# A hybrid encoder block on one core: where the adaLN products stand in the VectorE's list, and which steps of an attention head go first

## The chip, the core and the metric

The kernel runs on one core of a Trainium2 chip. A core has a TensorE (PE in the profile, with PEld for its weight loads), a VectorE (DVE), a ScalarE (ACT), a GpSimd (POOL, not used here but for a constant) and a SyncE (SP), which here issues all the transfers. Each engine works through a list of instructions of its own, in order; semaphores tie the lists together. The metric is the device time of one execution in microseconds.

## What is computed

One layer of an encoder with 256 positions, width 2048 and 16 heads of 128, all in float32:

```python
mod = silu(c) @ w_ada + b_ada
sh1, sc1, gt1, sh2, sc2, gt2, sh3, sc3, gt3 = split(mod, 9)
f = swiglu(modulate(rms_norm(h, g_ffn1), sh1, sc1), w1_gate, w1_up, w1_down)
h = h + 0.5 * gt1 * f
q, k, v = split(modulate(rms_norm(h, g_mix), sh2, sc2) @ w_qkv, 3)
# q and k normed; 8 heads of 2-D neighbourhood attention, 8 of dilated attention
h = h + gt2 * (concat(rms_norm(o_na), rms_norm(o_dil)) @ w_o)
f = swiglu(modulate(rms_norm(h, g_ffn2), sh3, sc3), w2_gate, w2_up, w2_down)
h = h + 0.5 * gt3 * f
```

The hidden width of both feed-forwards is 5632. With only 256 positions every weight is used on few columns, so the weights have to be streamed from memory once: 500 MB, 151 of them for `w_ada` alone.

## The kernel before

Weights come in chunks of 128 x 1024 (eight 128 x 128 blocks, 0.5 MB). To keep float32 accuracy a chunk is cut in two: ACT casts it to a rounded part `hi` (line 157), DVE subtracts it to leave the remainder `lo` (line 158; in the profile the tile is called low). PE then multiplies each block twice (`mm2`, lines 161 to 164): the rounded part by a rounded and a remainder part of the activations together (512 columns), the remainder by the rounded part alone (256 columns). `W.chunk` (lines 304 to 316) fetches and splits three chunks ahead of the one in use (`AHEAD`); raw chunks have five buffers, the two parts four each.

The adaLN vector `mod` is 144 columns of 128 values. Each column is one block of `w_ada`, 128 x 2048 or 1 MB. It does not pass through PE: the transfer (`ada_issue`, line 132) brings it, and one DVE instruction multiplies it by the broadcast of silu(c) and sums each row (`ada_use`, line 140). In the profile its tile is ra (two buffers) or rx (one more, outside attention). The blocks are spread thinly over the weight stream: each chunk that is fetched adds `ws.rate` to a credit, and at 1 a block is issued (lines 308 to 314). The rates are set by stage with `ws.pace`: `RA` and `RB` in the first feed-forward, `RQ` in attention, `RE` and `RF` in the second feed-forward. A block's transfer is kept behind that of the last chunk in SP's list (lines 133, 134); its product is written in the program when a later block needs its place in `pend` (`bg_step`, lines 254 to 258). `hold` keeps products behind the last step of a norm that PE waits for.

A planner arranges the lists: it takes instructions by priority, which is their place in the program, when its own estimate says that they can start. An instruction may so come out ahead of others that stand before it in the program. `high_priority(offset=n)` ranks the instructions within it as if they stood n places earlier. `after` (lines 116 to 120) adds an edge that the planner has to respect, without a semaphore when both are on one engine.

The stages are: first feed-forward (part of the up-projections ahead of time, the rest, down-projection, then the last 12 of 44 hidden blocks in the same way), attention, second feed-forward. In the second feed-forward the 64 chunks of `w2_a` run under `RE`, and 60 of the 64 of `w2_b` under `RF[0]`; `rest2` demands the modulation columns, `gate3` the gates.

In attention, 96 units of the q/k/v projection and 32 of the output projection run one after the other. PE's list there is written out by hand (`manual_schedule`); DVE and ACT are left to the planner. The steps of a head (`head`, lines 627 to 704) are hung on later units by a table `PLAN`: transposes of q and k (a_pe) and their split (a_ew), scores (b_pe), bias, maximum and exponentials (b_ew1), normalising (b_ew2), transposes of the probabilities (c_pe), their split (c_ew), the product with v (d_pe) and the output (d_ew). Norms of q and k (`qk_norm`) and sums of squares (`Stat`) feed the same engines.

Of the kernel before, what the change touches and what calls it, by code (L numbers as in the profile page):

```python
# [9 lines left out]
F32 = mybir.dt.float32  # L10
F32R = mybir.dt.float32r
AF = mybir.ActivationFunctionType
ALU = mybir.AluOpType
AX = mybir.AxisListType
# [24 lines left out]
RA = 0.475  # L39
RB = (0.28, 0.36, 0.36, 0.3)  # L40
RQ = 0.2
RE = 0.25
RF = (0.1, 0.2, 0.1, 0.1)
AHEAD = 3
RAWB = 5
ARA = 2
ARX = 1
LOB = 4
URGENT = 400
LINE = 16  # L50
PLACE = ((12, 36),) + 3 * ((16, 0),) + ((44, 40),) + 3 * ((48, 0),)
MANUAL = {mybir.EngineType.PE}
# [12 lines left out]
def build(tc, a):  # L65
    nc = tc.nc
    with ExitStack() as ctx:
# [44 lines left out]
        hold = []  # L112

        queue = []

        def after(ins, other, why):
            tc.add_manual_dep(
                ins.ins, other.ins.name,
                mybir.DependencyInfo(mybir.DependencyClass.NoSync, mybir.DependencyReason.DATA),
                reason=why)  # L120

        def held(ins):
            if hold:
                after(ins, hold[-1], "hold")

        def ada_issue(i):
            turn[0] += 1
            if wide and turn[0] % (ARA + ARX) >= ARA:
                raw = wide["p"].tile([P, D], F32, tag="arx", bufs=ARX, name=f"rx{i}")
            else:  # L130
                raw = wp.tile([P, D], F32, tag="ara", bufs=ARA, name=f"ra{i}")
            ins = nc.sync.dma_start(raw, a["w_ada"][i])
            if queue:
                after(ins, queue[-1], "queue")
            return raw

        def ada_use(raw, i):
            j, k = i // KT, i % KT
            m = mods[j][:, k : k + 1]
            held(nc.vector.tensor_tensor_reduce(  # L140
                out=raw, in0=raw, in1=cb, scale=1.0, scalar=vec[:, BA + i : BA + i + 1],
                op0=ALU.mult, op1=ALU.add, accum_out=m))
            if j in GAIN:
                g = vec[:, GAIN[j] + k : GAIN[j] + k + 1]
                nc.vector.scalar_tensor_tensor(m, m, 1.0, g, ALU.add, ALU.mult)
# [8 lines left out]
        def wsplit(raw, place):  # L154
            hi = wp.tile([P, CW + 64], F32R, tag="whi", bufs=LOB, name="hiw")[:, place[0] : place[0] + CW]
            lo = wp.tile([P, CW + 64], F32R, tag="wlo", bufs=LOB, name="low")[:, place[1] : place[1] + CW]
            nc.scalar.copy(hi, raw)  # L157
            nc.vector.tensor_tensor(lo, raw, hi.bitcast(F32), ALU.subtract)  # L158
            return hi, lo

        def mm2(out, lh, ll, r, first, last):
# [9 lines left out]
        def split(src, hi, lo):  # L171
            nc.scalar.copy(hi, src)
            nc.vector.tensor_tensor(lo, src, hi.bitcast(F32), ALU.subtract)
# [210 lines left out]
        def ffn(kx, part, ready_k, gate, rates, stat=None, out=None):  # L384


            hid = {}
            head = [pair("pb") for f in range(NF1)]
            ready_k(KM)
            for f in range(NF1):  # L390
                up_mm(head[f], kx, KM, True, False)
            ready_k(KT)
            ws.pace(rates[0])
            for f in range(NF1):
                up_mm(head[f], KM, KT, False, True)
                up_finish(f, head[f], part, hid)
            for f in range(NF1, F1):
                ps = pair("pb")
                up_mm(ps, kx, KT, True, True)
                up_finish(f, ps, part, hid)  # L400
            psum_pool("bank")
            ws.pace(rates[1])
            ffn_down(range(F1), hid, gate)
            psum_pool("pair")
            ws.pace(rates[2])
            for f in range(F1, FT):
                ps = pair("pb")
                up_mm(ps, 0, KT, True, True)
                up_finish(f, ps, {}, hid)
            ln_exp_set()  # L410
            psum_pool("bank")
            ws.pace(rates[3])
            ffn_down(range(F1, FT), hid, gate, stat, out)
# [92 lines left out]
        with tc.tile_pool(name="att", bufs=2) as ap_, tc.tile_pool(name="atc", bufs=1) as ac:  # L506
# [120 lines left out]
            def head(g, i, a0, b0, c0, d0):  # L627
                hd = g * 4 + i
                s_ = {}
                hs = slice(i * P, (i + 1) * P)  # L630

                def a_pe():
                    s_["pT"] = bank("pT")
                    for q, nm in enumerate(("k", "q")):
                        for t in range(2):
                            o_ = q * S + t * P
                            nc.tensor.transpose(s_["pT"][:, o_ : o_ + P], res[g, nm, t][:, i, :], ident)

                def a_ew():
                    s_["th"] = ap_.tile([P, 512], F32R, tag="th", name="th")  # L640
                    s_["tl"] = ap_.tile([P, 512], F32R, tag="tl", name="tl")
                    split(s_["pT"], s_["th"], s_["tl"])

                def b_pe():
                    th, tl = s_["th"], s_["tl"]
                    s_["ps"] = bank("psc").rearrange("p (t s) -> p t s", t=2)
                    for t in range(2):
                        qs = slice(S + t * P, S + (t + 1) * P)
                        mm3(s_["ps"][:, t, :], th[:, qs], tl[:, qs], th[:, 0:S], tl[:, 0:S], True, True)

                def b_ew1():
                    sc = ap_.tile([P, 2, S], F32, tag="sc", name="sc")
                    nc.vector.scalar_tensor_tensor(sc, s_["ps"], HD ** -0.5, s_["bias"], ALU.mult, ALU.add)
                    mx = sp.tile([P, 2], F32, tag="mx", name="mx")
                    nc.vector.tensor_reduce(mx, sc, axis=AX.X, op=ALU.max, negate=True)
                    sm = sp.tile([P, 2], F32, tag="sm", name="sm")
                    for t in range(2):
                        nc.scalar.activation(
                            sc[:, t, :], sc[:, t, :], AF.Exp, bias=mx[:, t : t + 1], accum_out=sm[:, t : t + 1])
                    s_["p"], s_["sm"] = sc, sm  # L660

                def b_ew2():
                    sc, sm = s_["p"], s_["sm"]
                    nc.vector.reciprocal(sm, sm)
                    for t in range(2):
                        if t < PACT:
                            nc.scalar.activation(sc[:, t, :], sc[:, t, :], AF.Copy, scale=sm[:, t : t + 1])
                        else:
                            nc.vector.tensor_scalar(sc[:, t, :], sc[:, t, :], sm[:, t : t + 1], None, ALU.mult)

                def c_pe():
                    s_["pP"] = bank("pP").rearrange("p (t s) -> p t s", t=2)
                    for t in range(2):
                        for kt in range(2):
                            nc.tensor.transpose(
                                s_["pP"][:, kt, t * P : (t + 1) * P], s_["p"][:, t, kt * P : (kt + 1) * P], ident)

                def c_ew():
                    s_["ph"] = ap_.tile([P, 2, S], F32R, tag="ph", name="ph")
                    s_["pl"] = ap_.tile([P, 2, S], F32R, tag="pl", name="pl")  # L680
                    split(s_["pP"], s_["ph"], s_["pl"])

                def d_pe():
                    s_["po"] = bank("po")[:, :S]
                    for kt in range(2):
                        vh, vl = res[g, "v", kt]
                        mm3(s_["po"], vh[:, hs], vl[:, hs], s_["ph"][:, kt, :], s_["pl"][:, kt, :],
                            kt == 0, kt == 1)

                def d_ew():  # L690
                    po = s_["po"]
                    go = vec[:, GO + hd : GO + hd + 1]
                    nc.scalar.activation(ox[hd][:, 0, :], po, AF.Copy, scale=go)
                    nc.vector.scalar_tensor_tensor(
                        ox[hd][:, 1, :], po, go, ox[hd][:, 0, :].bitcast(F32), ALU.mult, ALU.subtract)
                    ost[hd // 8].add(po, False)

                def fetch():
                    s_["bias"] = na_bias(hd) if g < 2 else lnc

                at(max(0, a0 - 2), fetch)
                for u, fn in ((a0, a_pe), (a0 + 1, a_ew), (b0, b_pe), (b0 + 1, b_ew1), (b0 + 2, b_ew2),
                              (c0, c_pe), (c0 + 1, c_ew), (d0, d_pe), (d0 + (0 if d0 == LAST else 1), d_ew)):
                    at(u, fn)
# [161 lines left out]
```

## Time and profile before

| | |
|---|---|
| median of three runs | 1928.16 us (1927.46 to 1933.04) |
| the profiled execution | 1929.37 us, of which the span of its instructions 1927.4 us |
| granted clock of the TensorE, mean over the span | 0.993 |
| memory traffic | 500.09 MB read, 261 GB/s over the span |
| first feed-forward, PE at work | 22 to 769 us |
| attention, projections and output projection | 776 to 1191 us |
| second feed-forward | 1196 to 1924 us |

The profile is that of one execution. A group of it gives line, engine, operation, tile written <- tiles read, shape and count, then busy time and the mean of one in ns, then the idle time of the engine ahead of these instructions and what ended it. The list of waits gives who waited for whom: total, times, longest. The timeline gives start and length of each instruction, those alike put together, with the wait ahead of the first in square brackets. The start of one matmul to that of the next is the better measure of PE, since their ends overlap.

### The profile page before, as it was taken

To read this page: it belongs to the slowest core of one execution; us is meant where nothing else is said; L and a number is where in the kernel's file an instruction comes from. 1 tells how busy PE (TensorE), PEld (TensorE's weight loads), DVE (VectorE), ACT (ScalarE), POOL (GpSimd) and SP (SyncE) were. 2 spreads that over 40 slices of the span, in tenths; PEclk is the share of its full clock that TensorE was granted. 3 is DMA by queue.
4 is the path that set the end of the run, shared out by engine and by line. 5 is a ranking of instruction groups with operands and counts; after the bars stand their busy time and mean duration, and the time that the engine had idled before them with its cause. 6 is when DMAs were issued, how large, how long until landed. Compare 5 with 4: busy or idle time off the path is not lost.

```text
span 1927.4 us, 27567 instructions
## 1 busy us (share of the span) xinstructions
PE 1885.8 (98%) x10564; PEld 1639.3 (85%) x10564; DVE 1565.1 (81%) x2122; ACT 906.8 (47%) x1333; POOL 0.7 (0%) x6
## 2 busy tenths in 40 slices
PE   7999999999999999999999999999999999999999
PEld 5878888888888888887878788888888888888888
DVE  7899999988888889868876799788798976665665
ACT  2444544543334454555555465545454443334442
POOL 0000000000000000000000000000000000000000
PEclk8999999999999999999999999999999999999999
DMA  9998888789998887776755445787677677766664
GB/s 384 383 332 292 299 299 296 295 323 338 330 332 327 312 306 256 246 286 222 263 189 194 145 141 164 273 304 286 230 234 235 210 251 273 260 228 191 193 203 136
DMA packets 120227, 503.98 MB, mean 261 GB/s; under 512 B 13344, under 2 KB 15904, under 8 KB 101664
## 3 DMA queue, kind: packets, MB, share of 16 engines
q1 hardware_dynamic: 120096, 502.24, 74.5%
q8 instruction: 82, 1.34, 0.3%
q14 instruction: 49, 0.40, 0.1%
HBM read 500.09 MB, written 2.10 MB: 261 GB/s over the span
## 4 chain that ended last, share of the span: by engine, by line
PE 85%; DVE 8%; DMA 3%; issue 2%; ACT 2%; SPq 0%; DVEq 0%; ACTq 0%
PE pb L163 20%; PE pd L163 17%; PE pb L164 10%; PE pd L164 8%; PE pa L163 8%; PE pqk L169 4%; PE pa L164 4%; PE pqv L169 3%; DVE low L158 3%; PE pqq L169 3%; DMA ra<-in_w_ada_dram 2%; PE pa L462 2%; PE pso L163 2%; ACT hiw L157 1%; PE pso L164 1%
## 5 line engine op out<-in xcount | busy, mean ns | idle before, releaser
L157 ACT CAST hiw<-rw 128x1024 fp32r<-128x1024 f32 x644 | 674.2, 1049 | 705.1 <-PE pd L163 234.0
L158 DVE TENSOR_TENSOR low<-rw,hiw 128x1024 fp32r<-128x1024 f32 x644 | 782.0, 1221 | 186.5 <-ACT hiw L157 184.5
L163 PE MATMUL pb<-nx,hiw 128*128 128x512 f32 x1920 | 657.4, 390 | 0.0
L164 PE MATMUL pb<-nx,low 128*128 128x256 f32 x1920 | 532.1, 277 | 1.1 <-DVE low L158 1.1
L163 PE MATMUL pd<-hd,hiw 128*128 128x512 f32 x1408 | 481.9, 390 | 0.0
L163 PEld LDWEIGHTS pb<-nx,hiw 128*128 128x128 f32 x1920 | 360.5, 188 | 76.9
L164 PE MATMUL pd<-hd,low 128*128 128x256 f32 x1408 | 390.1, 277 | 1.8 <-DVE low L158 1.8
L164 PEld LDWEIGHTS pb<-nx,low 128*128 128x128 f32 x1920 | 360.9, 188 | 1.9 <-DVE low L158 1.9
L163 PEld LDWEIGHTS pd<-hd,hiw 128*128 128x128 f32 x1408 | 264.3, 188 | 56.3
L140 DVE CUSTOM_DVE_ANT_0 ra<-ra,cb,vec 128x2048 f32<-128x2048 f32 x101 | 237.2, 2349 | 75.2 <-DMA ra<-in_w_ada_dram 75.0
L163 PE MATMUL pa<-nx,hiw 128*128 128x512 f32 x800 | 276.1, 392 | 3.7 <-ACT hiw L157 3.2
L164 PEld LDWEIGHTS pd<-hd,low 128*128 128x128 f32 x1408 | 264.6, 188 | 2.6 <-DVE low L158 2.4
L164 PE MATMUL pa<-nx,low 128*128 128x256 f32 x800 | 221.6, 279 | 4.0 <-DVE low L158 4.0
L163 PEld LDWEIGHTS pa<-nx,hiw 128*128 128x128 f32 x800 | 149.6, 188 | 37.2 <-ACT hiw L157 5.2
L164 PEld LDWEIGHTS pa<-nx,low 128*128 128x128 f32 x800 | 150.4, 188 | 8.9 <-DVE low L158 7.9
L140 DVE CUSTOM_DVE_ANT_0 rx<-rx,cb,vec 128x2048 f32<-128x2048 f32 x43 | 101.0, 2348 | 28.6 <-DMA rx<-in_w_ada_dram 28.3
L163 PE MATMUL pso<-ox,hiw 128*128 128x512 f32 x256 | 92.4, 404 | 0.0
L169 PE MATMUL pqk<-hiw,nx 128*128 128x512 f32 x256 | 85.5, 400 | 0.0
L169 PE MATMUL pqq<-hiw,nx 128*128 128x512 f32 x256 | 84.3, 399 | 0.0
L169 PE MATMUL pqv<-hiw,nx 128*128 128x512 f32 x256 | 81.5, 393 | 0.3 <-ACT nx L232 0.3
L378 DVE SCALAR_TENSOR_TENSOR h<-pd,m,h 128x256 f32<-128x256 f32 x128 | 61.2, 481 | 16.5 <-PE pd L164 14.7
L164 PE MATMUL pso<-ox,low 128*128 128x256 f32 x256 | 72.5, 283 | 0.0
(133 smaller groups left out, 1513.5 us busy)
## 6 DMA issues: line engine op xcount, KB each, us to landing
ra<-in_w_ada_dram SPq DMA_DIRECT2D x101, 1024.0 KB, 7.4
rw<-in_w_b_dram SPq DMA_DIRECT2D x144, 512.0 KB, 4.6
rw<-in_w_d_dram SPq DMA_DIRECT2D x128, 512.0 KB, 5.2
rw<-in_w_a_dram SPq DMA_DIRECT2D x100, 512.0 KB, 4.8
rw<-in_w_c_dram SPq DMA_DIRECT2D x96, 512.0 KB, 4.4
rw<-in_w_qkv_dram SPq DMA_DIRECT2D x96, 512.0 KB, 4.3
rx<-in_w_ada_dram SPq DMA_DIRECT2D x43, 1024.0 KB, 7.3
rw<-in_w_e_dram SPq DMA_DIRECT2D x48, 512.0 KB, 4.4
```

What stands on the lines that cost most here:

```text
L140: held(nc.vector.tensor_tensor_reduce(out=raw, in0=raw, in1=cb, scale=1.0, scalar=vec[:, BA + i : BA + i + 1], op0=ALU.mult, op1=ALU.add, ...
L157: nc.scalar.copy(hi, raw)
L158: nc.vector.tensor_tensor(lo, raw, hi.bitcast(F32), ALU.subtract)
L163: nc.tensor.matmul(out, lh, r, start=first, stop=False)
L164: nc.tensor.matmul(out[:, :S], ll, r[:, 0, :], start=False, stop=last)
L169: nc.tensor.matmul(out, l, r, start=first and i == 0, stop=last and i == 2, **kw)
L378: nc.vector.scalar_tensor_tensor(h[d], part_, g, h[d], ALU.mult, ALU.add)
L462: nc.tensor.matmul(pa[f][:, q, :], w[:, b * P : (b + 1) * P], full[k], start=k == 0 and q == 0, stop=k == K1 - 1 and q == 1, skip_group_ch ...
```

## The change

It has three parts.

1. `wsplit` keeps the last two remainders in `lows`. From the point in the first feed-forward where `late` is set, a block that is issued takes along `lows[0]`, the remainder of the chunk before the one fetched last, and its product gets an edge behind that remainder.
2. Four of a head's element-wise steps (a_ew, b_ew1, b_ew2, c_ew) are put in `high_priority(offset=SOON)`, with `SOON = 60`. The step d_ew is not.
3. In the second feed-forward `RE` is 0.28 in place of 0.25, and `RF[0]` is 0.2 in place of 0.1.

```diff
-RE = 0.25
-RF = (0.1, 0.2, 0.1, 0.1)
+RE = 0.28
+RF = (0.2, 0.2, 0.1, 0.1)
+SOON = 60
...
+        lows = []
+        late = []
...
             ins = nc.sync.dma_start(raw, a["w_ada"][i])
             if queue:
                 after(ins, queue[-1], "queue")
-            return raw
+            return raw, lows[0] if late and lows else None
 
         def ada_use(raw, i):
             j, k = i // KT, i % KT
             m = mods[j][:, k : k + 1]
-            held(nc.vector.tensor_tensor_reduce(
+            raw, low = raw
+            ins = nc.vector.tensor_tensor_reduce(
                 out=raw, in0=raw, in1=cb, scale=1.0, scalar=vec[:, BA + i : BA + i + 1],
-                op0=ALU.mult, op1=ALU.add, accum_out=m))
+                op0=ALU.mult, op1=ALU.add, accum_out=m)
+            held(ins)
+            if low is not None:
+                after(ins, low, "landing")
...
-            nc.vector.tensor_tensor(lo, raw, hi.bitcast(F32), ALU.subtract)
+            lows[:] = lows[-1:] + [nc.vector.tensor_tensor(lo, raw, hi.bitcast(F32), ALU.subtract)]
             return hi, lo
...
             ready_k(KT)
+            late[:] = [True]
             ws.pace(rates[0])
...
                 def a_ew():
-                    s_["th"] = ap_.tile([P, 512], F32R, tag="th", name="th")
-                    s_["tl"] = ap_.tile([P, 512], F32R, tag="tl", name="tl")
-                    split(s_["pT"], s_["th"], s_["tl"])
+                    with tc.high_priority(offset=SOON):
+                        s_["th"] = ap_.tile([P, 512], F32R, tag="th", name="th")
+                        s_["tl"] = ap_.tile([P, 512], F32R, tag="tl", name="tl")
+                        split(s_["pT"], s_["th"], s_["tl"])
...
```

The bodies of b_ew1, b_ew2 and c_ew are indented under the same line; nothing else in them changes.

More of the change, by code (lines that the diff above doesn't have):

```diff
@@ L651, in b_ew1 @@
                 def b_ew1():
[L652 to L659, printed above, removed]
@@ L660, in b_ew1 @@
-                    s_["p"], s_["sm"] = sc, sm
-                def b_ew2():
[L663 to L669, printed above, removed]
+                    with tc.high_priority(offset=SOON):
+                        sc = ap_.tile([P, 2, S], F32, tag="sc", name="sc")
+                        nc.vector.scalar_tensor_tensor(sc, s_["ps"], HD ** -0.5, s_["bias"], ALU.mult, ALU.add)
+                        mx = sp.tile([P, 2], F32, tag="mx", name="mx")
+                        nc.vector.tensor_reduce(mx, sc, axis=AX.X, op=ALU.max, negate=True)
+                        sm = sp.tile([P, 2], F32, tag="sm", name="sm")
+                        for t in range(2):
+                            nc.scalar.activation(
+                                sc[:, t, :], sc[:, t, :], AF.Exp, bias=mx[:, t : t + 1], accum_out=sm[:, t : t + 1])
+                        s_["p"], s_["sm"] = sc, sm
@@ new lines, in b_ew2 @@
+                def b_ew2():
+                    with tc.high_priority(offset=SOON):
+                        sc, sm = s_["p"], s_["sm"]
+                        nc.vector.reciprocal(sm, sm)
+                        for t in range(2):
+                            if t < PACT:
+                                nc.scalar.activation(sc[:, t, :], sc[:, t, :], AF.Copy, scale=sm[:, t : t + 1])
+                            else:
+                                nc.vector.tensor_scalar(sc[:, t, :], sc[:, t, :], sm[:, t : t + 1], None, ALU.mult)
@@ L678, in c_ew @@
                 def c_ew():
-                    s_["ph"] = ap_.tile([P, 2, S], F32R, tag="ph", name="ph")
-                    s_["pl"] = ap_.tile([P, 2, S], F32R, tag="pl", name="pl")
-                    split(s_["pP"], s_["ph"], s_["pl"])
+                    with tc.high_priority(offset=SOON):
+                        s_["ph"] = ap_.tile([P, 2, S], F32R, tag="ph", name="ph")
+                        s_["pl"] = ap_.tile([P, 2, S], F32R, tag="pl", name="pl")
+                        split(s_["pP"], s_["ph"], s_["pl"])
                 def d_pe():
```

## The prediction

> **What bounds the kernel now.** I read the page first, then the stretches by stage, then the list of waits, then the timelines around each place where the TensorE (PE) stood still.
>
> ```profile
> PE 1885.8 (98%) x10564; PEld 1639.3 (85%) x10564; DVE 1565.1 (81%) x2122; ACT 906.8 (47%) x1333; POOL 0.7 (0%) x6
> PE 85%; DVE 8%; DMA 3%; issue 2%; ACT 2%; SPq 0%; DVEq 0%; ACTq 0%
> L158 DVE TENSOR_TENSOR low<-rw,hiw 128x1024 fp32r<-128x1024 f32 x644 | 782.0, 1221 | 186.5 <-ACT hiw L157 184.5
> L140 DVE CUSTOM_DVE_ANT_0 ra<-ra,cb,vec 128x2048 f32<-128x2048 f32 x101 | 237.2, 2349 | 75.2 <-DMA ra<-in_w_ada_dram 75.0
> ```
>
> PE is the bound: busy 98%, 85% of the chain that ended last. Nothing in the change removes PE work, so all there is to gain is the few per cent in which PE waits. DVE is the engine that makes it wait. Its two large jobs are the remainder of a weight chunk (L158, 1.22 us) and the product of an adaLN block (L140, 2.35 us). The product also made DVE stand idle 75 us for its own transfer, and DVE takes its instructions in the order of its list: what stands behind a waiting product waits too. Which stages does that hurt?
>
> ```profile
> 182.00:396.00 214.00, 214.00 (x1252) 188.81 (x1251) 206.53 (x280) 107.55 (x142) 0.00 (x0) 1.00 0.82 293
> 396.00:571.00 175.00, 175.00 (x1026) 154.44 (x1025) 145.71 (x162) 68.66 (x68) 0.00 (x0) 1.00 0.92 335
> 1100.00:1191.00 91.00, 86.47 (x522) 76.37 (x521) 84.39 (x164) 52.69 (x102) 0.00 (x0) 0.99 0.53 168
> 1380.00:1546.00 166.00, 165.60 (x967) 145.77 (x966) 151.32 (x223) 85.06 (x121) 0.00 (x0) 1.00 0.68 221
> 1546.00:1721.00 175.00, 173.18 (x1010) 152.32 (x1009) 116.78 (x125) 67.57 (x67) 0.00 (x0) 1.00 0.72 258
> ```
>
> Columns: stretch, its length, then busy time of PE, its weight loads, DVE, ACT and POOL, PE's clock, DMA share, GB/s. In the first feed-forward (182 to 571) PE is busy all the time, though DVE is busy 206.53 of 214 us: nothing can be won there. In the second one (1380 to 1721) 0.40 and 1.82 us are missing. The rest is between 776 and 1192, in attention. The waits of that stretch, then those of 1380 to 1721 (total, times, longest, us):
>
> ```profile
> PE pP L675 <- DVE sc L669: 5.9, 3, 2.6
> PE pT L637 <- DVE qn L569: 2.9, 1, 2.9
> PE pstat L221 <- ACT sq L209: 2.1, 2, 1.1
> PE po L169 <- DVE pl L173: 1.4, 1, 1.4
> ```
>
> ```profile
> DVE ra L140 <- DMA ra<-in_w_ada_dram: 33.0, 10, 5.0
> DVE rx L140 <- DMA rx<-in_w_ada_dram: 17.7, 5, 5.2
> PEld pd L164 <- DVE low L158: 2.4, 2, 1.3
> PE pd L164 <- DVE low L158: 1.8, 2, 1.0
> PEld pb L164 <- DVE low L158: 0.7, 1, 0.7
> PE pb L164 <- DVE low L158: 0.4, 1, 0.4
> ```
>
> In attention PE waits for a head's softmax (sc), for its split (pl), for a norm (qn) and for a square (sq). In the second feed-forward it waits three times for a remainder.
>
> **The products (first part).** A product now stays in DVE's list behind the remainder of the chunk before the one that was fetched last when its block was issued. I counted the order in the timelines of SP and DVE: of the 112 blocks issued from 192 us on, 13 products stand there already, 65 stand one remainder ahead of it, 33 two and one three. So 99 move by one to three remainders. No instruction is added. The place where it matters most, DVE first, then SP:
>
> ```profile
> 1698.00 2.35 DVE L140 CUSTOM_DVE_ANT_0 ra<-ra,cb,vec 128x2048 f32<-128x2048 f32 x1 [4.97 <-DMA ra<-in_w_ada_dram]
> ...
> 1700.68 3.48 DVE L158 TENSOR_TENSOR low<-rw,hiw 128x1024 fp32r<-128x1024 f32 x3
> ```
>
> ```profile
> 1690.43 0.42 SPq L132 DMA_DIRECT2D ra<-in_w_ada_dram  x1
> ```
>
> The block is issued at 1690.43 and lands 7.57 us later; DVE idles 4.97 us for it, works 2.35, and the remainders behind it begin at 1700.68, after PE has asked for the first. With the change two of these three remainders run in the idle stretch and the product follows about when it lands: the wait goes, and the queue behind it is no longer late. All three waits of PE here have this form. By the PE rows they cost 2.2 us, by the weight loads 3.1; I take 2.7. What is late next is nothing near: the remainders are then a chunk or two ahead. What the new order queues behind is only a product, and who waits for a product is its adaLN column, used much later, and its buffer: the block that reuses it is issued three blocks on at 0.36 a chunk or two blocks on at 0.2, at least 8 chunks of 175 / 64 = 2.73 us, 22 us. The remainder that now precedes the product ends 9 to 15 us after the block's issue in this trace, and 2.35 more make 17, so SP's list is not held. In the first feed-forward 54 products move too, for nothing, since PE loses nothing there now.
>
> The first of the three softmax waits has the same cause (DVE, then PE):
>
> ```profile
> 863.86 0.68 DVE L655 TENSOR_REDUCE mx<-sc 128x2 f32<-128x512 f32 x1
> 868.23 2.35 DVE L140 CUSTOM_DVE_ANT_0 ra<-ra,cb,vec 128x2048 f32<-128x2048 f32 x1 [3.69 <-DMA ra<-in_w_ada_dram]
> ...
> 872.30 0.60 DVE L669 TENSOR_SCALAR sc<-sc,sm 128x256 f32<-128x256 f32 x2
> ```
>
> ```profile
> 869.67 0.62 PE L169 MATMUL pqk<-hiw,nx 128*128 128x512 f32 x2
> ...
> 870.35 0.39 PE L169 MATMUL pqk<-hiw,nx 128*128 128x512 f32 x1
> 872.79 0.82 PE L675 MATMUL pP<-ident,sc 128*128 128x128 f32 x4 [2.06 <-DVE sc L669]
> 873.26 0.78 PE L169 MATMUL pqk<-hiw,nx 128*128 128x512 f32 x1
> ...
> 876.40 0.45 PE L169 MATMUL pqk<-low,nx 128*128 128x512 f32 x1
> ```
>
> The normalising step waited behind a product that waited 3.69 us for its transfer. Matmuls start every 0.228 us before (0.68 us for 3); from 870.35 to 872.79 PE loses 2.44 - 0.23 = 2.21 us. Then seven matmuls take 3.14 us from 873.26 to 876.40 in place of 1.60: another 1.54 at a lower clock. This place costs 3.75 us.
>
> [...]
>
> **The heads' precedence (second part).** Splits, softmax and normalising of a head rank as if written 60 instructions earlier, ahead of remainders not yet needed. It adds nothing either; the order of PE is fixed by hand and stays. The second softmax wait, DVE, then PE:
>
> ```profile
> 979.94 2.35 DVE L140 CUSTOM_DVE_ANT_0 ra<-ra,cb,vec 128x2048 f32<-128x2048 f32 x1
> ...
> 984.46 0.68 DVE L653 SCALAR_TENSOR_TENSOR sc<-psc,nab 128x512 f32<-128x512 f32 x1
> ...
> 991.09 0.61 DVE L669 TENSOR_SCALAR sc<-sc,sm 128x256 f32<-128x256 f32 x2
> ```
>
> ```profile
> 988.55 0.39 PE L169 MATMUL pqq<-hiw,nx 128*128 128x512 f32 x1
> 991.58 0.63 PE L675 MATMUL pP<-ident,sc 128*128 128x128 f32 x4 [2.65 <-DVE sc L669]
> ...
> 992.50 1.00 PE L169 MATMUL pqq<-hiw,nx 128*128 128x512 f32 x2
> ...
> 995.86 0.45 PE L169 MATMUL pqq<-low,nx 128*128 128x512 f32 x1
> ```
>
> The chain lasts 7.24 us from 984.46 to 991.70. Its own DVE work is 0.68 (sc), 0.68 (mx, as in the row above) and 0.61, together 1.97; two exponentials of ACT lie in it, and the rest is remainders and norms of another chain in between, after a product held DVE to 982.29. The exponentials would have to take 7.24 - 1.97 - 2.65 = 2.62 us for the wait to stay once the rest is out of the way, and the product's going adds to that. Price: 3.03 - 0.23 = 2.80, and 3.36 for eight starts in place of 1.82: 4.34 us. The third softmax wait is what is left of 5.9: 1.2 us, no product near it. The wait for pl (1.4) is a split behind a remainder. Both should go. The squares' 2.1 us are two waits; the earlier follows a product that now moves, but the square itself gets no precedence: between 0 and 1.0, I take 0.5. The 2.9 us for qn stay, since neither edit touches the norms.
>
> What the precedence costs is not in the trace: remainders slip by up to a head's steps. Below, zero; above, a wait of PE like the worst here, 4.34. I take one like the pl wait, 1.4, the nearest row of an instruction that is merely out-ranked.
>
> **The rates (third part).** 0.25 to 0.28 in the first stage of the second feed-forward moves its last blocks some 7 chunks earlier: nothing. 0.1 to 0.2 in the next stage (1380 to 1546) puts 0.1 x 60 chunks = 6 more blocks there, which leave the later stage. Each needs 2.35 us of DVE: 151.32 + 14.1 = 165.4 of 166 us. That is tight. If none of the idle time could be used it costs 14.1, if all, 0. I take 0: products rank last, and 182 to 396 ran at 96.5% DVE without a wait of PE. SP's list gets 6 issues sooner; transfers rise by 1.05 MB x 0.1 per 2.73 us, 221 to about 260 GB/s, where 396 to 571 carried 335.
>
> **Sum.** 2.7 + 3.75 + 4.34 + 1.2 + 1.4 + 0.5 = 13.9, less 1.4: 12.5 us. The profiled execution took 1929.4 (span 1927.4 and 2.0 around it), 1.2 above the median of 1928.16; from the median, **1915.7 us**.
>
> **Rivals.**
> - Precedence does not reach far enough: the second and third softmax waits and pl stay (4.34 + 1.2 + 1.4, without the allowance). Gain 7.0: 1921.2. For it: part of what stands in the way are norms of another chain. Chance 0.17.
> - DVE becomes the bound at 1380 to 1546: half of 14.1 lost, 1922.8. For it: 165.4 of 166. Chance 0.09.
> - The clock stays low where it is low now: 2 x 1.54 remain, 1918.8. Against it: the low rate starts behind the gaps. Chance 0.04. [...]
> - The qn wait goes as well, by a new order of DVE, with a slow stretch like 1.54 behind it: 4.4 more, 1911.3. Chance 0.06.
> - The change does not take hold, or new waits eat the gain: 1928. Chance 0.06.
> - Slower: heads' steps push remainders past their use while DVE is full (84.39 of 91 us at 1100 to 1191). Sixteen heads could each do it; at 4.34 a time it takes three to undo the gain and more than four (12.5 + 5.8 over 4.34) to be slower by 0.3%. Six: 1941.7. Against it: remainders lie two or three chunks ahead of use. Chance 0.05.
>
> The forecast keeps 0.53. A measurement of this kernel tells about 0.3%, 5.8 us, from no change: faster means below 1922.4. That is the forecast 0.53, most of the first rival 0.12, half of the second 0.04, the clock 0.04 and the norm 0.06: 0.79. Slower 0.05, the rest 0.16. The range runs from 1909.5 (norm wait gone and no allowance: 1909.9) to 1924.5, past the DVE rival.
>
> **What would show it.** Right: no DVE wait over 1 us at L140 for a transfer behind 776 us; no wait of PE for sc, pl, or a remainder; 1380 to 1721 at full PE; the qn wait still there. Wrong: PE waiting for low in attention or before 1546, DVE full there, or new waits for tl, ph or pl.

## The result, and the profile after

The changed kernel takes 1912.66 us (median of 4 runs, 1911.07 to 1914.06), the kernel before 1927.81 us beside it (4 runs). The ratio is 0.9914, with a 95% interval of 0.9896 to 0.9932: faster by 0.9%, 15.2 us by the medians. The forecast was 1915.7 us, a gain of 12.5. The profiled execution took 1911.73 us with a span of 1910.0, 17.4 us less than the span before; the profile of before was of an execution a little above its median and this one of an execution a little below, so the two profiles show some 2 us more than the runs do.

The page of the changed kernel (L165 is now the remainder, L144 the product, L176 the products in attention):

```profile
PE 1876.7 (98%) x10564; PEld 1633.8 (86%) x10564; DVE 1563.4 (82%) x2122; ACT 907.5 (48%) x1333; POOL 0.7 (0%) x6
PE 92%; DVE 5%; ACT 1%; DMA 1%; issue 1%; SPq 0%; ACTq 0%; DVEq 0%
L165 DVE TENSOR_TENSOR low<-rw,hiw 128x1024 fp32r<-128x1024 f32 x644 | 785.5, 1222 | 271.4 <-ACT hiw L164 269.8
L144 DVE CUSTOM_DVE_ANT_0 ra<-ra,cb,vec 128x2048 f32<-128x2048 f32 x101 | 236.9, 2345 | 4.9 <-DMA ra<-in_w_ada_dram 4.9
```

PE and DVE run as many instructions as before (10564 and 2122). The product in ra made DVE idle 4.9 us for its transfer where it was 75.0, all of it before 776 us. DVE's idle time did not vanish: ahead of the remainders it rose from 186.5 to 271.4 us, and what ends it is the ACT's cast, whose own idle time ends for the most part (539 of 726 us) when PE is done with something. So more of DVE's waiting is now for the bound engine, and less of the bound engine's is for DVE. PE's share of the last chain rose from 85 to 92%.

PE's busy time fell too, by 9.1 us, though it runs the same matmuls: at a granted clock of 0.50 a matmul counts as busy for longer (0.63 us in the last section's rows for what takes 0.40 at 1.00). The granted clock, taken over the span, rose from 0.993 to 0.996. The last section shows where it was low.

Busy time by stretch (length, PE, PEld, DVE, ACT, POOL, clock, DMA share, GB/s), first-feed-forward stages, then the up- and the down-projection of the second one:

```profile
182.00:396.00 214.00, 214.00 (x1253) 188.97 (x1252) 206.84 (x280) 107.44 (x143) 0.00 (x0) 1.00 0.83 295
396.00:571.00 175.00, 175.00 (x1025) 154.56 (x1025) 144.30 (x159) 68.24 (x68) 0.00 (x0) 1.00 0.91 332
...
1366.00:1532.00 166.00, 166.00 (x973) 146.66 (x973) 161.85 (x235) 86.43 (x123) 0.00 (x0) 1.00 0.77 267
1532.00:1707.00 175.00, 175.00 (x1026) 154.65 (x1025) 106.59 (x113) 68.07 (x68) 0.00 (x0) 1.00 0.69 219
```

The last two lines stand for 1380 to 1546 and 1546 to 1721 before. PE has no gap left there, with DVE at 161.85 of 166 us.

By the first matmul of each stage, attention with both projections took 776.2 to 1196.0 before (419.8 us) and 776.1 to 1182.3 now (406.2): 13.6 us of the 17.4. The second feed-forward and the end took 731.4 and now 727.7: 3.7. What PE still waits for in attention (770 to 1185; total, times, longest):

```profile
PE pT L645 <- DVE qn L577: 3.1, 2, 2.7
PE pstat L227 <- DVE sqa L224: 2.9, 2, 1.8
...
PE pstat L228 <- DVE sq L214: 1.0, 1, 1.0
...
PE pa L170 <- DVE nx L240: 0.9, 1, 0.9
```

No softmax and no pl is left. The norm (qn) is, as forecast. The sums of squares (sqa, sq) and the first norm of the second feed-forward (nx) are at the ends of dependent chains.

### The profile page after: what moved, and what is told of

The parts are those of the page before. It is cut to its first block, busy times and chain, and to the rows that moved or that the text cites. A ratio compares the mean times of both kernels' runs of the same rounds, so it can differ in the third digit from the quotient of the medians.

```text
span 1910.0 us, 27533 instructions
## 1 busy us (share of the span) xinstructions
PE 1876.7 (98%) x10564; PEld 1633.8 (86%) x10564; DVE 1563.4 (82%) x2122; ACT 907.5 (48%) x1333; POOL 0.7 (0%) x6
## 4 chain that ended last, share of the span: by engine, by line
PE 92%; DVE 5%; ACT 1%; DMA 1%; issue 1%; SPq 0%; ACTq 0%; DVEq 0%
PE pb L170 23%; PE pd L170 17%; PE pb L171 12%; PE pd L171 8%; PE pa L170 8%; PE pqk L176 5%; PE pqq L176 5%; PE pa L171 4%; PE pqv L176 4%; PE pa L470 2%; PE pso L170 2%; DVE low L165 2%; PE pso L171 1%; DVE ra L144 1%; DMA ra<-in_w_ada_dram 1%
## 5 line engine op out<-in xcount | busy, mean ns | idle before, releaser
L165 DVE TENSOR_TENSOR low<-rw,hiw 128x1024 fp32r<-128x1024 f32 x644 | 785.5, 1222 | 271.4 <-ACT hiw L164 269.8
L144 DVE CUSTOM_DVE_ANT_0 ra<-ra,cb,vec 128x2048 f32<-128x2048 f32 x101 | 236.9, 2345 | 4.9 <-DMA ra<-in_w_ada_dram 4.9
L144 DVE CUSTOM_DVE_ANT_0 rx<-rx,cb,vec 128x2048 f32<-128x2048 f32 x43 | 100.9, 2346 | 1.2 <-DMA rx<-in_w_ada_dram 1.2
L176 PE MATMUL pqk<-hiw,nx 128*128 128x512 f32 x256 | 84.3, 395 | 0.0
L176 PE MATMUL pqq<-hiw,nx 128*128 128x512 f32 x256 | 83.0, 393 | 0.0
L176 PE MATMUL pqv<-hiw,nx 128*128 128x512 f32 x256 | 81.4, 392 | 0.3 <-ACT nx L239 0.3
```

The costliest lines, as they stand in the source:

```text
L144: ins = nc.vector.tensor_tensor_reduce(out=raw, in0=raw, in1=cb, scale=1.0, scalar=vec[:, BA + i : BA + i + 1], op0=ALU.mult, op1=ALU.add, ...
L165: lows[:] = lows[-1:] + [nc.vector.tensor_tensor(lo, raw, hi.bitcast(F32), ALU.subtract)]
L176: nc.tensor.matmul(out, l, r, start=first and i == 0, stop=last and i == 2, **kw)
```

## The experiments

Three runs put one part of the change alone into the kernel before, a fourth leaves one part out. Each was timed against the kernel before on the same chip.

**The order of the products alone.** `RE`, `RF` and the heads as before; `lows`, `late` and the edge of the changed kernel:

```diff
-            return raw
+            return raw, lows[0] if late and lows else None
...
+            if low is not None:
+                after(ins, low, "landing")
...
+            lows[:] = lows[-1:] + [nc.vector.tensor_tensor(lo, raw, hi.bitcast(F32), ALU.subtract)]
...
+            late[:] = [True]
```

> The products' order alone (part 1); heads and rates as before. My theory: it takes the three remainder waits of the second feed-forward (2.7 to 3.1 us) and the first softmax wait (3.75 us) and helps the wait for the square at 1002 (0.5 to 1.7 us); the second and third softmax waits and the pl wait stay. Gain 7 to 9 us, about 1920 us. Rival (the precedence does nearly all of attention): only the second feed-forward is gained, 3 us, 1925 us. Both: no wait of DVE over about 1 us at L144 for a transfer behind 776 us.

Measured: 1917.39 us (5 runs), ratio 0.9938 (0.9923 to 0.9952). More than the theory gave it: some 12 us against 1929.01 in that series. The waits of PE between 785 and 1172 us:

```profile
PE pT L645 <- DVE qn L577: 3.1, 2, 2.7
PE pP L683 <- DVE sc L677: 2.3, 3, 1.2
PE po L176 <- DVE pl L180: 1.4, 1, 1.4
PE pstat L228 <- ACT sq L216: 1.1, 1, 1.1
```

The first softmax wait is gone, the pl wait stays and so does the third softmax wait (1.2), as expected. But the second, 4.34 us in the forecast and counted there for the heads' precedence, has shrunk to 0.69 lost at 985.7, and one of two waits for a square is gone. A small new one of 0.77 stands at 910. Between 1360 and 1712 PE waits for no remainder.

**The heads' precedence alone.** `SOON` as in the change; products and rates as before. Against the changed kernel, with `late` empty no edge is made:

```diff
-RE = 0.28
-RF = (0.2, 0.2, 0.1, 0.1)
+RE = 0.25
+RF = (0.1, 0.2, 0.1, 0.1)
...
-            late[:] = [True]
```

> The heads' precedence alone (part 2); products and rates as before. My theory: second and third softmax waits and the pl wait go (4.34 + 1.2 + 1.4 = 6.9 us), the first softmax wait stays, since a product that waits for its transfer still stands in front, and the waits of the second feed-forward stay. About 1921 us. Rival: with a maximum and exponentials that come a remainder earlier, the first normalising step gets ahead of the product as well; then all of attention is gained by this part alone, about 11 us, 1917 us. Second rival: without the order of part 1 the second wait stays, since a product of 2.35 us still holds DVE ahead of sc: 1925 us.

Measured: 1918.75 us (6 runs), ratio 0.9943 (0.9929 to 0.9958). DVE, then PE, around the first softmax:

```profile
865.62 0.68 DVE L664 TENSOR_REDUCE mx<-sc 128x2 f32<-128x512 f32 x1
870.79 2.35 DVE L144 CUSTOM_DVE_ANT_0 ra<-ra,cb,vec 128x2048 f32<-128x2048 f32 x1 [4.49 <-DMA ra<-in_w_ada_dram]
...
873.07 0.16 DVE L674 RECIPROCAL sm<-sm 128x2 f32<-128x2 f32 x1
...
874.27 0.61 DVE L679 TENSOR_SCALAR sc<-sc,sm 128x256 f32<-128x256 f32 x2
```

```profile
872.12 0.39 PE L176 MATMUL pqk<-hiw,nx 128*128 128x512 f32 x1
874.76 0.63 PE L685 MATMUL pP<-ident,sc 128*128 128x128 f32 x4 [2.26 <-DVE sc L679]
875.15 0.48 PE L176 MATMUL pqk<-hiw,nx 128*128 128x512 f32 x1
875.46 0.39 PE L176 MATMUL pqk<-low,nx 128*128 128x512 f32 x1
```

Precedence decides who goes into DVE's list first, and does nothing once a waiting product is in front: this one waits 4.49 us for its transfer, and PE's wait of 2.26 us stays. The second and third softmax waits and pl are gone, so the rivals fall. The time alone would not have told: it lies midway between the theory's 1921 and the first rival's 1917. The waits for remainders stay in the second feed-forward (2.1 us in three), and a new one of 0.9 us stands at 845.

**The rates alone.** `late` stays empty here too, and the heads are as before:

```diff
-RE = 0.25
-RF = (0.1, 0.2, 0.1, 0.1)
+RE = 0.28
+RF = (0.2, 0.2, 0.1, 0.1)
```

> The rates alone (part 3); products and heads as before. My theory: nothing, 1928 us within 2; the waits for remainders shift from the stage of the down-projection into that of the up-projection (before about 1546), where more products now wait for their transfers. Rival (DVE is the bound there): twelve products of 2.35 us and their waits of 1 to 3 us in a stage where DVE has 14.7 us to spare push remainders late, 1932 to 1942 us.

Measured: 1924.51 us (12 runs, 1919.62 to 1928.52), ratio 0.9979 (0.9967 to 0.9991): a little faster, where both theories had no gain or a loss. In its profile the three waits for remainders are down to one of 0.7 us, since four products are left in the down-projection, where there were eleven: some 2 us. The rest is not settled; in this one profile no slow matmuls follow the qn wait, which is worth 2.7 us against the profile of before (see the last section), but one profile doesn't tell how often that happens.

**Everything but the rates.** Against the changed kernel:

```diff
-RE = 0.28
-RF = (0.2, 0.2, 0.1, 0.1)
+RE = 0.25
+RF = (0.1, 0.2, 0.1, 0.1)
```

> Parts 1 and 2 without the rates. My theory: the same time as the changed kernel, 1912.7 us within 2; DVE less busy from 1370 to 1540, more in the down-projection behind it, PE at full in both. Rival: the rates carried part of the gain (the second feed-forward gained 3.7 us, the three waits were worth 2.7 to 3.1), then 1914 to 1916 us.

Measured: 1912.15 us (5 runs), ratio 0.9915 (0.9900 to 0.9930): the same as the changed kernel. With the products in order there is nothing left that the rates could gain.

**How far is DVE from its limit?** First with more blocks in the up-projection; the edits from here on are against the changed kernel.

```diff
-RF = (0.2, 0.2, 0.1, 0.1)
+RF = (0.27, 0.2, 0.1, 0.1)
```

> The changed kernel with RF[0] = 0.27, so that all 16 gate blocks are issued in the 60 chunks after 1366 us. DVE then has 161.9 + 4 x 2.35 = over 166 of 166 us to do there, if it takes all products in that stretch. My theory (products rank last, so they slip behind and remainders do not suffer): PE stays at 166 of 166, products run up to five remainders past their edge and some end in the down-projection, 1912.7 us within 2. Rival (DVE is the bound once it is full): 5 to 10 us of waits for low in that stretch, 1918 to 1923 us.

Measured: 1919.87 us (8 runs), ratio 0.9951 (0.9935 to 0.9967). The rival's size, but not its place: from 1366 to 1532 PE is busy 165.60 of 166 us while the products slip, up to eight remainders past their edge. The debt falls due at the end of the stage, where the last two almost follow one another (DVE):

```profile
1544.54 2.34 DVE L144 CUSTOM_DVE_ANT_0 rx<-rx,cb,vec 128x2048 f32<-128x2048 f32 x1
...
1547.15 2.34 DVE L144 CUSTOM_DVE_ANT_0 ra<-ra,cb,vec 128x2048 f32<-128x2048 f32 x1
...
1549.76 1.21 DVE L165 TENSOR_TENSOR low<-rw,hiw 128x1024 fp32r<-128x1024 f32 x1
```

PE has been asking for that remainder since 1546.8 and loses 4.0 us, then 2.6 more in slowed matmuls (5.50 us from 1551.02 to 1556.52 for what takes 2.89 in the changed kernel); with 0.56 at 1521 that makes the 7.2 by which it is above the changed kernel's 1912.66.

Then, with the same blocks, the products' last rank is taken away too.

```diff
-            ins = nc.vector.tensor_tensor_reduce(
+            with tc.high_priority(offset=URGENT if j == 8 else 0):
+                ins = nc.vector.tensor_tensor_reduce(
```

> As the run before, and the products of the gate blocks rank 400 instructions earlier, so they run right behind the remainder of their edge instead of last. This takes the cover away. My theory: PE now waits for remainders or for finished hidden blocks in that stretch; DVE has about 11 us too much to do, less two chunks of lead: 3 to 10 us, 1916 to 1922 us. Rival (order does not matter as long as nothing waits for its transfer): 1912.7 us within 2.

Measured: 1923.35 us (12 runs), ratio 0.9968 (0.9955 to 0.9981). Now each product stands right behind its edge, and nearly each makes PE wait 0.3 to 0.6 us, most of them 0.6 to 0.9 us by the starts of the matmuls (1360 to 1712):

```profile
PE pb L172 <- DVE low L166: 4.1, 11, 0.6
PE pb L171 <- ACT hiw L165: 0.6, 1, 0.6
PE pd L172 <- DVE low L166: 0.4, 1, 0.4
```

So the last rank is worth something even where DVE is full, 3.5 us by the medians, though the runs of the two overlap. At 0.2 the products with their last rank cost nothing; what they would cost there in front was not run.

**Where the edge stands.** One remainder earlier:

```diff
-            lows[:] = lows[-1:] + [...]
+            lows[:] = lows[-2:] + [...]
```

> The changed kernel with the edge one remainder earlier (the last but two in place of the last but one). Products then stand one remainder further ahead, about 2.7 us sooner: 7 to 10 us after their issue where a block lands 7.0 to 7.5 us (median) after it. My theory: a few waits of DVE for transfers come back, each up to 1 us, too short to reach PE: 1912.7 within 2. Rival (the exact place matters): the first softmax wait or a wait for a remainder returns, 1915 to 1920 us.

Measured: 1911.7 us (6 runs), ratio 0.9911 (0.9893 to 0.9930). The products' waits for transfers grew from 4.9 + 1.2 to 18.8 + 5.9 us over the span, none reached PE. One remainder more or less does not count, as long as no product waits for long: behind 776 us the longest such wait is now 1.3 us, in the kernel before it was 5.2.

**The norms.** What the change left alone, the qn wait, was tried with the same precedence.

```diff
+            def soon(fn, *args):
+                with tc.high_priority(offset=SOON):
+                    fn(*args)
...
-at(u + 1, lambda: qk_squares(nm, ps, st_))
+at(u + 1, lambda: soon(qk_squares, nm, ps, st_))
```

The root (qk_rstd) and the norm (qk_norm) are called through `soon` in the same way.

> The changed kernel with the same precedence of 60 for the squares, the root and the norm of q and k. My theory: the wait of the transposes for qn at 1082 (2.9 us and 0.9 us of slower matmuls behind it) and the short one at 1006 (0.5 us) go: 1908.4 us within 2. Rival (these steps now take the place of the heads' own): another wait of the same size, 1912.7 us.

Measured: 1913.0 us (6 runs), ratio 0.9915 (0.9897 to 0.9933): no gain, the rival is right. The waits from 785 to 1172:

```profile
PE pstat L227 <- DVE sqa L224: 4.7, 1, 4.7
PE pT L649 <- DVE qn L581: 0.2, 1, 0.2
```

The qn wait is gone, and the wait for the sum of the heads' squares has grown from 1.8 to 4.7 us: the last heads' output steps (d_ew), which have no precedence, come behind casts, remainders and the output projection's own steps.

**Norms and a head's last step.** To the edit of the norms the whole body of d_ew is added:

```diff
                 def d_ew():
+                    with tc.high_priority(offset=SOON):
...
```

> The changed kernel with the precedence of 60 for the norms of q and k and also for a head's last step (d_ew: output, its remainder, the square for the sum). In the run with the norms alone the wait for qn went, but the sum of squares at 1122 waited 4.8 us, since the last heads' output steps had a remainder and other work ahead of them. My theory: both go but for what the last head itself needs after its product, 1.3 us: 2.9 + 0.9 + 0.5 + 0.6 us less than the changed kernel, 1908 us within 2. Rival (the work that is out-ranked turns up as a third wait): 1912.7 us.

Measured: 1908.83 us (4 runs, 1908.27 to 1909.60), ratio 0.9900 (0.9885 to 0.9915).

```profile
PE pstat L228 <- ACT sq L216: 1.7, 1, 1.7
PE po L176 <- DVE pl L180: 0.4, 1, 0.4
PE pT L649 <- DVE qn L581: 0.2, 1, 0.2
```

The qn wait is gone without a successor of its size; what is left is the last head's own chain and a little of pl. This version is faster than both kernels, by 3.8 us against the changed one by the medians; their runs do not overlap, though they are of different series.

Then d_ew alone, without the norms:

> The changed kernel with the precedence of 60 for a head's last step alone. My theory: the wait for the sum of squares at 1125 falls from 1.9 to 1.3 us, the wait for qn stays at 2.9: 1912 us within 2. Rival (d_ew in front delays the norms of q): the qn wait grows, 1914 us.

Measured: 1912.60 us (4 runs), ratio 0.9919 (0.9905 to 0.9933). As expected: the wait at the sum is 1.2, qn stays at 2.7. Only both together pay.

**The reach of the precedence.**

```diff
-SOON = 60
+SOON = 15
```

> The changed kernel with SOON = 15 in place of 60: about one unit of the program in place of three or four. My theory: with the products out of the way one unit is enough for most, and the third softmax wait or the pl wait returns at most: 1912.7 to 1915.5 us. Rival (the reach makes no difference): the same waits as in the changed kernel, 1912.7 us; second rival (nothing is left of the precedence): as with the order alone, 1917.4 us.

Measured: 1914.38 us (5 runs), ratio 0.9930 (0.9917 to 0.9942). In the profile the softmax waits stay away and the pl wait is back with 1.2 us, as the theory had it; in time this is 1.7 us above the changed kernel, within what the intervals leave open.

## Why the prediction held, point by point

**The products.** Right in mechanism. In the second feed-forward the three waits for remainders went, and the stage gained 3.7 us where 2.7 were set. The last product but two of that stage shows the new order (DVE of the changed kernel):

```profile
1554.33 1.23 DVE L165 TENSOR_TENSOR low<-rw,hiw 128x1024 fp32r<-128x1024 f32 x1 [1.49 <-ACT hiw L164]
1557.06 1.22 DVE L165 TENSOR_TENSOR low<-rw,hiw 128x1024 fp32r<-128x1024 f32 x1 [1.50 <-ACT hiw L164]
1558.20 2.34 DVE L144 CUSTOM_DVE_ANT_0 ra<-ra,cb,vec 128x2048 f32<-128x2048 f32 x1
```

The remainders run when ACT has their rounded part, the product follows and waits for nothing. In the first feed-forward, where products moved too, nothing was gained, as said. The first softmax wait (3.75) belongs to this part alone: it is gone with the order alone and there with the precedence alone.

**The heads.** The term of 4.34 us for the second softmax wait was booked on the precedence. The runs show that either part removes nearly all of it: with the order alone 0.69 is left, with the precedence alone nothing. The forecast had seen both causes, a product of 2.35 us and the work of other chains, but had not asked whether one of them was enough. The same holds for the square at 1004: 0.5 was taken between 0 and 1.0, and with either part the whole wait went, 1.3 us by the starts. These shared terms are why the parts do not add: 1 - 0.9938 and 1 - 0.9943 make 1.19%, both together 0.85% without the rates. The difference is 6.6 us; 3.65 of the softmax and 1.3 of the square account for 5.0. Each of the ratios is known to some 0.15%, 3 us, so the rest says nothing. The third softmax wait and pl (1.2 and 1.4) belong to the precedence alone.

**The allowance.** 1.4 us were set for new waits. They came, in other places: 0.5 at a qn transpose at 1006 and 0.7 more at the heads' sum of squares. The 0.9 us for nx ahead of the second feed-forward are no new cost: from the matmul behind the wait for sq to the first one of that stage it takes 4.77 us, and 5.29 before, where the granted clock was 0.50 from 1190.53 to 1193.94. The matmuls after the remaining qn wait lost 1.2 us, in the profile of before 2.7 (the sums are in the last section). So what the allowance stood for came out as about 1 us gained. No head step pushed a remainder late in the changed kernel, so the slower rival was far off.

**The rates.** Zero was right with the other two parts. The six more products are there (5 before, 11 now), but DVE's load, set at 165.4 of 166, came out at 161.85. The forecast added lengths of rows to a busy time, and rows that follow one another without idle time overlap: above, the remainder at 1557.06 lasts 1.22 us and the product starts 1.14 after it, and behind a product the next instruction starts after 2.27 us, not 2.35. Products slipped up to four remainders past their edge. The rival (DVE the bound) was near: at 0.27 it costs 7 us.

**The clock.** The rival, by which the clock stays low where it was low, fell in its outcome: in the changed kernel no slow matmuls remain at the two places. But the forecast's reading, that they belong to the gap, was too simple, as the last section shows: behind a qn wait of 2.7 to 3.0 us there were slow matmuls in eight of eleven profiles and none in three. The forecast's sum holds 2 x 1.54 us of them because its one profile had them at both places, and in that it was lucky.

**The size.** 13.9 less 1.4 was forecast. By the medians 15.2 came, by the two profiles 17.4. Of the 4.9 us that the profiles show beyond the forecast, 0.8 are the square, 1.0 the second feed-forward, 0.4 the softmax waits and pl together, and some 2.5 the allowance, which was not needed. The stated range, 1909.5 to 1924.5, held.

## What to carry to other kernels

When an engine takes its list in order, look for instructions in it that stand ready behind one that waits for a transfer; an ordering edge that costs nothing, placed where the transfer has surely landed, gives the waiting time back (DVE idled 75.0 us for ra here, then 4.9), and one chunk more or less did not matter. Background work should also rank last (worth some 3.5 us here where the engine was full), and its engine should keep a few per cent of room: at 161.85 of 166 us nothing was lost, four blocks more cost 7 us at the stage's end. Precedence moved a wait to what was left without it (2.7 us at qn gone, 1.8 to 4.7 at the sum of squares): it paid on the norms only together with the step that took their place in the queue, so look for the next wait before counting a gain, and try parts alone before adding their gains up. And a wait of the TensorE that is read from one profile may cost its length or more: at the first softmax wait 2.21 us were lost in the gap and 3.75 with the slow matmuls behind it, in another run's profile none was slow there, so read the clock beside it.

## What was not expected of the hardware

The TensorE's clock after a short gap. Where PE stood still for 2 to 3 us, the matmuls behind it either ran at about half the rate for a while (0.64 us a pair below, in place of 0.35) or did not slow at all. In the kernel before, a wait of 2.06 us was followed by seven slow matmuls. With the precedence alone, the same place had a wait of 2.26 us, and the rows above show none: 875.15 to 875.46, then the normal 0.23 us a start. PE behind the qn wait of the changed kernel (start, length, and in brackets the idle time before it):

```profile
1085.07 0.48 PE L645 MATMUL pT<-ident,qn 128*128 128x128 f32 x1 [2.74 <-DVE qn L577]
1085.20 0.77 PE L170 MATMUL pso<-ox,hiw 128*128 128x512 f32 x1
...
1085.99 0.63 PE L170 MATMUL pso<-ox,hiw 128*128 128x512 f32 x1
...
1086.63 0.63 PE L170 MATMUL pso<-ox,hiw 128*128 128x512 f32 x1
...
1087.27 0.63 PE L170 MATMUL pso<-ox,hiw 128*128 128x512 f32 x1
...
1087.88 0.40 PE L170 MATMUL pso<-ox,hiw 128*128 128x512 f32 x1
...
1088.23 0.40 PE L170 MATMUL pso<-ox,hiw 128*128 128x512 f32 x1
```

One pair of matmuls takes 0.79 us, then 0.64, 0.64 and 0.61, and from there 0.35. Where nothing is slow, as in the run without the rates, the first pair takes 0.42 and the others 0.35 from the start, so four slow pairs cost 1.2 us. In the kernel before the first takes 0.79 and eight follow at 0.64: 2.7 us. The same wait stands in eleven profiles, each time 2.7 to 3.0 us long, and the number of slow pairs behind it was 0 in three of them, 4 to 6 in six and 9 in two.

The granted clock stands beside it. These are two stretches of 3.41 us around the first softmax wait, first in the kernel before, then with the precedence alone (columns as above: the second number behind the stretch is PE's busy time, the third from the end the clock):

```profile
869.68:873.09 3.41, 1.35 (x8) 0.88 (x7) 3.41 (x8) 1.04 (x1) 0.00 (x0) 1.00 0.15 37
873.09:876.50 3.41, 3.41 (x12) 2.74 (x11) 3.41 (x5) 0.59 (x1) 0.00 (x0) 0.50 0.74 217
```

```profile
870.60:874.01 3.41, 1.91 (x9) 1.25 (x7) 3.22 (x4) 1.38 (x2) 0.00 (x0) 1.00 0.34 139
874.01:877.42 3.41, 2.65 (x14) 2.30 (x15) 3.41 (x7) 0.59 (x1) 0.00 (x0) 1.00 0.57 150
```

PE stood still for 2.06 us of the first stretch in the kernel before, and the clock of the second was 0.50. With the precedence alone it stood still for 1.50 us of the first and 0.76 of the second, and the clock was 1.00 in both.

From 27 to 1907 us the clock was 0.50 at four places in the kernel before, 873.09 to 876.50, 992.56 to 995.97, 1094.96 to 1101.78 and 1190.53 to 1193.94, and at one in the changed kernel, 1084.41 to 1087.82. The waits of PE there were 2.06, 2.65 and 2.92 us, a pair of 1.10 and 1.01, and 2.74. The three qn waits without slow matmuls, with the rates alone, with everything but the rates and with `SOON = 15`, lasted 2.95, 2.76 and 2.74 us. The pair of 1.10 and 1.01 us stands in the changed kernel too, at 1175 to 1178, with the clock at 1.00. So the length of the wait did not tell the two kinds apart, and what does is not shown here.

The clock also differs from run to run of one kernel, and its longest executions may owe part of their time to it. In one series of the kernel before (1922.30 to 1936.76, 19 runs) the two slowest runs had a granted clock of 0.991 and 0.992 over the span, the two fastest 0.996 and 0.997. The clock is not all of it: one run at 0.996 took 1932.82. The changed kernel, with fewer such gaps, spread over 3 us, but in 4 runs only.
